# A one-hot matrix on TensorE in place of the first expert's gather

## The chip, the core and the metric

The kernel runs on one core of one Trainium2 chip. Its engines have their own instruction queues and go through them strictly in order: PE (TensorE) does matrix products, DVE (VectorE) and ACT (ScalarE) work on elements, POOL (GpSimd) does a little arithmetic and issues the indirect DMAs, SP (SyncE) issues the weight loads. The metric is the device time of one execution in microseconds (us).

## The reference

Two layers of a streaming encoder, each with three parts. Only the third part, a mixture of experts, matters here:

```python
scores = softmax(xt @ w_router + b_router)
# best group of 4 experts by the sum of its top-2 scores, then the top-2 experts in it
gate = sum(one_hot(eid, N_EXPERTS) * top_w[..., None], axis=1)
for e in range(N_EXPERTS):                       # 16 experts
    h = silu(xt @ w_gate[e]) * (xt @ w_up[e])
    y = y + gate[:, e:e + 1] * (h @ w_down[e])
x = layer_norm(DN_ALPHA * x + y)
```

xt has 512 tokens of 1024 numbers, and each token goes to two of the sixteen experts.

## The kernel before

The 512 tokens are four tiles of 128 rows, xr[0] to xr[3], in fp32. Products are made of fp16 halves: a number is scaled and split into a high half (ACT copies it to fp16, L124 or L173) and a low half (DVE subtracts the high half, L129 or L174), and three products stand for one fp32 product (`mm3`, L168 to L170).

Weights come from DRAM as units of 1 MB. `Feed` loads them in order into raw buffers (`fill`, L98, on SP's queue), and `pump` splits the next raw unit into `whi` and `wlo`. There are 4 raw buffers of the kind "b", 7 of the kind "x" and 2 of the kind "y" in this part of a layer, and 5 pairs of halves. A pair is free once PE has used it (`done`), a raw buffer once it is split. So PE frees pairs, ACT and DVE split into them, and SP loads into the raw buffers that this frees.

The stretch of the change is the passage from attention to the experts, once in each layer. `OutProj` makes the output projection tile by tile and the layer norm behind it (`ln0`, `ln`, L331 to L342). For each finished tile `x3T(t)` (L931) stores the rows to the DRAM copy `xd`, transposes them on PE and splits the result, and `logits(t)` multiplies with the router's weights. `route()` (L965) then picks the experts: some thirty small DVE operations, with one round of rank products on PE (L992, L993) that number the tokens of each expert; `pc` (L1001) holds each token's slot in its expert, `ohs` (L1005) is a one-hot matrix of the slots, 96 (`CAP`) wide.

What follows stands in this order for every engine: `tokens()` makes the list of tokens of each expert on PE and DVE (`idxT`, L1024); `fetch(0)`, `fetch(1)` and `fetch(2)` gather the rows of the first three experts from `xd` by indirect DMA on POOL (L1137); one `feed.pump(1)`; `gates(pc)` (L1030) makes the gate weights, sixteen DVE operations; `dispatch(0)` (L1152) transposes the gathered rows on PE and splits them into `xgh` and `xgl` (L1160, L173, L174); `out_rows()` (L1053) makes the rows and gates of the output on PE (`slots`, L1016) and DVE; then comes expert 0's `gate_up` (L1169).

`idle(real, rest, other)` fills PE while it would wait: in layer 0 with `real` products of the next layer's V projection (48 in all, L371; `v_end` does those that are left and splits the result), in layer 1 with `other` products that nobody reads (`warm`, L185).

Of the kernel before, what the change touches and what calls it, by code (L numbers as in the profile page):

```python
# [10 lines left out]
F16 = mybir.dt.float16  # L11
# [3 lines left out]
OP = mybir.AluOpType  # L15
# [19 lines left out]
SC = SW * SX  # L35
ISC = 1.0 / SC
RAW_B, HL_B = 4, 4
RAW_X, HL_X, RAW_Y = 7, 1, 2
YEND = 4
BIG = 4096.0  # L40
UPL = 30 + 6 * NE
# [3 lines left out]
def trunk_kernel(ctx, tc, units, xT, x, memT, alow, wa2, b_a, gn_g, w_sT, b_s, slnT,  # L45
# [20 lines left out]
    class Feed:  # L66
        def __init__(self):
            self.items = []
            self.raw = {}
            self.hl = {}  # L70
            self.nload = 0
            self.nsplit = 0
            self.rawfree = deque("b" * RAW_B)
            self.hlfree = deque("b" * HL_B)
            self.px = self.px2 = self.ph = None
            self.limit = 1 << 30

        def add(self, src, scale=SW, dest=None, cols=2048):
# [11 lines left out]
        def fill(self, eng=nc.sync):  # L90
            while self.nload < min(len(self.items), self.limit):
                k = self.slot(self.rawfree, self.nload)
                if k is None:
                    return
                src, _, _, cols = self.items[self.nload]
                pl, b = {"b": (ring, RAW_B), "x": (self.px, RAW_X), "y": (self.px2, RAW_Y), "mem": (cp, 1)}[k]
                t = pl.tile([P, 2048], F32, tag="mem" if k == "mem" else "raw", bufs=b, name=nm("raw"))
                eng.dma_start(t[:, :cols], src)  # L98
                self.raw[self.nload] = (t, k)
                self.nload += 1  # L100
# [205 lines left out]
    def transpose_x(t, hi, lo):  # L306
        for g in range(2):
            p = ps()
            for j in range(4):
                pe.transpose(p[:, j * P:(j + 1) * P], xr[t][:, (4 * g + j) * P:(4 * g + j + 1) * P], ident)  # L310
            split_ps(hi[:, 4 * g:4 * g + 4], lo[:, 4 * g:4 * g + 4],
                     p.rearrange("p (j s) -> p j s", j=4), SX)
# [114 lines left out]
    for l in range(DEPTH):  # L427
# [441 lines left out]
        with ExitStack() as ex:  # L869
# [2 lines left out]
            feed.ph = phc.__enter__()  # L872
            pxc = tc.tile_pool(name=f"px{l}", bufs=1, reuse_waits="tile")
            feed.px = pxc.__enter__()
            fin = l == DEPTH - 1
            feed.xend = {"h": u["end"], "x": u["end"] - (8 if fin else 0), "y": u["end"] - (8 if fin else YEND), "mem": u["end"]}
            feed.limit = u["end"] + 4
            feed.rawfree.extend("x" * RAW_X)
            if fin:
# [27 lines left out]
            def lay(n):  # L907
                used[0] += n
                return scr[:, used[0] - n:used[0]]
# [21 lines left out]
            def x3T(t):  # L931
                nc.scalar.dma_start(xd[t * P:(t + 1) * P, :], xr[t])
                x3hl = (ep if t % 2 else x3p).tile([P, 2, KT, P], F16, tag="xg2" if t % 2 else "x3", name=nm("x3"))
                x3[t] = (x3hl[:, 0], x3hl[:, 1])
                transpose_x(t, *x3[t])

            def logits(t):
                x3h, x3l = x3[t]
# [26 lines left out]
            def route():  # L965
                dve.tensor_reduce(c[:, :, 0], sc, axis=AX.X, op=OP.max)
                dve.tensor_tensor(sc, sc, b16(c[:, :, 0]), op=OP.subtract)
                act.activation(sc, sc, AF.Exp)
                v = sc.rearrange("p t (g e) -> p (t g) e", g=4)
                pair = lay(96).rearrange("p (g i) -> p g i", g=16)  # L970
                dve.tensor_tensor(pair[:, :, 0:3], v[:, :, 0:3], v[:, :, 1:4], op=OP.add)
                dve.tensor_tensor(pair[:, :, 3:5], v[:, :, 0:2], v[:, :, 2:4], op=OP.add)
                dve.tensor_tensor(pair[:, :, 5:6], v[:, :, 0:1], v[:, :, 3:4], op=OP.add)
                gs = small(4)
                dve.tensor_reduce(gs.rearrange("p t g -> p (t g)"), pair, axis=AX.X, op=OP.max)
                beats(zw, v)
                beats(zg, gs)
                we = wins(zw, 16)
                wg = wins(zg, NT)
                t2 = small(NE)  # L980
                tv = t2.rearrange("p t (g e) -> p (t g) e", g=4)
                gsel = scs[:, 5 * NE:6 * NE].rearrange("p (t n) -> p t n", t=NT)
                dve.scalar_tensor_tensor(gsel, wg, -1.0, th[:, 0:4], op0=OP.add, op1=OP.is_equal)
                dve.tensor_tensor(tv, we, th, op=OP.is_ge)
                gb = gsel.rearrange("p t g -> p (t g)").unsqueeze(2).to_broadcast([P, 16, 4])
                sv = sel.rearrange("p t (g e) -> p (t g) e", g=4)
                dve.tensor_tensor(sv, tv, gb, op=OP.mult)
                p = ps()
                for t in range(NT):
                    o = p[:, t * NE:(t + 1) * NE]  # L990
                    for t0 in range(t):
                        pe.matmul(o, ones16, sel[:, t0], start=(t0 == 0), stop=False)  # L992
                    pe.matmul(o, stri, sel[:, t], start=(t == 0), stop=True)  # L993
                dve.tensor_tensor(tv, we, th, op=OP.is_equal)
                dve.tensor_tensor(ch[:, 1].rearrange("p t (g e) -> p (t g) e", g=4), tv, gb, op=OP.mult)
                dve.tensor_tensor(ch[:, 0], sel, ch[:, 1], op=OP.subtract)

                used[0] = 0
                pc = lay(2 * NT * NE).rearrange("p (c x) -> p c x", c=2)
                for i in range(2):  # L1000
                    dve.scalar_tensor_tensor(pc[:, i], p[:, :NT * NE], 1.0,  # L1001
                                             ch[:, i].rearrange("p t e -> p (t e)"), op0=OP.add, op1=OP.mult)
                pch = lay(2 * NT)
                dve.tensor_reduce(pch, pc.rearrange("p c (t e) -> p (c t) e", t=NT), axis=AX.X, op=OP.add)
                dve.tensor_tensor(ohs, iot.unsqueeze(1).to_broadcast([P, 2 * NT, CAP]),  # L1005
                                  pch.unsqueeze(2).to_broadcast([P, 2 * NT, CAP]), op=OP.is_equal)
                for i in range(2):
                    dve.tensor_tensor(aux[:, i, 0], ch[:, i], b16(rid), op=OP.mult)
                return pc

            def slots(ohc, auxc, n):

# [112 lines left out]
            feed.rawfree.extend("y" * (RAW_Y - 1))  # L1125
            feed.fill()
            idle(15, 0, 15)
            pc = route()

            scat = []  # L1130

# [97 lines left out]
            def down(e, after=None):  # L1229
# [5 lines left out]
                scatter(o, idxR[:CAP, e:e + 1])  # L1235
                del E[e]

            idle(9, 0, 6)
            tokens()
            fetch(0)  # L1240
            fetch(1)
            feed.rawfree.append("y")
            feed.fill(pool)
            fetch(2)
            feed.pump(1)
            gates(pc)
            idle(11, 0, 17)
            dispatch(0)
            idle(3, 3, 3)
            v_end()  # L1250
            out_rows()
            if fin:
# [98 lines left out]
            if not fin:  # L1351
                ln_open()
                load_ln(l, 2)
                down(NE - 1)
                pxc.__exit__(None, None, None)
                phc.__exit__(None, None, None)
                with tc.tile_pool(name=f"ovf{l}", bufs=1, reuse_waits="tile") as fp:
                    overflow(fp)
            else:

                pxc.__exit__(None, None, None)
                ln_open()
                load_ln(l, 2)
# [163 lines left out]
```

## Time and profile before

| | us |
|---|---|
| median of 3 runs | 1289.42 (1288.48 to 1290.34) |
| the profiled execution, its own time | 1289.44 |
| its span in the trace | 1287.8 |
| PE busy in the span | 1175.2 (91%) |
| DVE busy in the span | 912.2 (71%) |
| ACT busy in the span | 711.9 (55%) |

The profiled execution's own time is 1.6 us above its span, and lies 0.02 us from the median of the runs. Times in the rows are counted from the start of the span. Layer 0's passage to the experts lies at about 340 to 376 us, layer 1's at about 972 to 1006 us. A timeline row gives start, duration, engine, line and operation, what is written and read, and how many such operations were merged; in brackets stands how long the engine was idle before it and what ended that.

### The profile page before, as it was taken

To read this page: it belongs to the slowest core of one execution; us is meant where nothing else is said; L and a number is where in the kernel's file an instruction comes from. 1 tells how busy PE (TensorE), PEld (TensorE's weight loads), DVE (VectorE), ACT (ScalarE), POOL (GpSimd) and SP (SyncE) were. 2 spreads that over 40 slices of the span, in tenths; PEclk is the share of its full clock that TensorE was granted. 3 is DMA by queue.
4 is the path that set the end of the run, shared out by engine and by line. 5 is a ranking of instruction groups with operands and counts; after the bars stand their busy time and mean duration, and the time that the engine had idled before them with its cause. 6 is when DMAs were issued, how large, how long until landed. Compare 5 with 4: busy or idle time off the path is not lost. (4 is left out here: it accounts for less than half of the span.)

```text
span 1287.8 us, 26082 instructions
## 1 busy us (share of the span) xinstructions
PE 1175.2 (91%) x11218; PEld 763.4 (59%) x11219; DVE 912.2 (71%) x1066; ACT 711.9 (55%) x810; POOL 235.9 (18%) x193
## 2 busy tenths in 40 slices
PE   6999999999979999999859999999998899999982
PEld 4455456464457777777645545444644777777761
DVE  3255775378578989989574275773758699899977
ACT  3435334344447888888543354232633678888873
POOL 3002000000331222231150002000004222222124
PEclk9999999999988999999879999999999899999996
DMA  9412225228569999999472231155374899999864
GB/s 360 159 67 98 98 85 178 98 98 316 208 238 345 419 418 418 418 419 394 165 291 105 98 129 36 67 207 184 110 313 142 292 377 419 417 419 418 337 235 181
DMA packets 54940, 314.76 MB, mean 244 GB/s; under 512 B 9309, under 2 KB 9405, under 8 KB 22560
## 3 DMA queue, kind: packets, MB, share of 16 engines
q1 hardware_dynamic: 42096, 279.99, 55.3%
q0 software_dynamic: 11568, 28.83, 6.2%
q10 hardware_dynamic: 1152, 4.19, 0.8%
q8 instruction: 90, 1.47, 0.5%
q14 instruction: 34, 0.28, 0.1%
HBM read 302.80 MB, written 22.68 MB: 253 GB/s over the span
## 5 line engine op out<-in xcount | busy, mean ns | idle before, releaser
L129 DVE SCALAR_TENSOR_TENSOR wlo<-raw,whi 128x2048 f16<-128x2048 f32 (+1 forms) x234 | 523.2, 2278 | 110.5 <-ACT whi L124 109.5
L124 ACT ACTIVATE whi<-raw 128x2048 f16<-128x2048 f32 (+1 forms) x239 | 441.8, 1895 | 34.7 <-PE ps L170 19.4
L169 PE MATMUL ps<-xgl,whi 128*128 128x96 f16 x2048 | 272.4, 208 | 21.8 <-DVE xgl L174 21.7
L168 PE MATMUL ps<-xgh,whi 128*128 128x96 f16 x2048 | 274.3, 208 | 5.0 <-ACT xgh L173 2.9
L170 PE MATMUL ps<-xgh,wlo 128*128 128x96 f16 x2048 | 272.6, 208 | 0.3 <-issue 0.3
L170 PEld LDWEIGHTS <-wlo 128*128 128x128 f16 x2400 | 237.8, 99 | 58.7 <-issue 25.7
L169 PEld LDWEIGHTS <-whi 128*128 128x128 f16 x2400 | 237.8, 99 | 39.2 <-issue 9.5
L168 PEld LDWEIGHTS <-whi 128*128 128x128 f16 x2400 | 238.1, 99 | 38.3 <-issue 6.7
L1143 POOL DMA_INDIRECT y<-rows,idxR x31 | 59.7, 1927 | 353.0 <-ACT rows L1233 345.0
L168 PE MATMUL ps<-whi,xT 128*128 128x512 f16 (+1 forms) x256 | 91.9, 359 | 8.4 <-ACT whi L124 7.0
L170 PE MATMUL ps<-whi,xT 128*128 128x512 f16 (+1 forms) x256 | 91.7, 358 | 3.1 <-DVE xT L174 2.2
L169 PE MATMUL ps<-wlo,xT 128*128 128x512 f16 (+1 forms) x256 | 91.7, 358 | 1.7 <-DVE wlo L129 1.7
L168 PE MATMUL ps<-whi,hhl 128*96 128x512 f16 x200 | 75.9, 380 | 2.3 <-ACT hhl L1202 2.3
L170 PE MATMUL ps<-whi,hhl 128*96 128x512 f16 x200 | 75.9, 379 | 0.0
L169 PE MATMUL ps<-wlo,hhl 128*96 128x512 f16 x200 | 75.8, 379 | 0.0
L294 ACT ACTIVATE lnmv<-lnmv,c_lneps 128x1 f32<-128x1 f32 x16 | 4.7, 295 | 111.0 <-DVE lnmv L293 111.0
L1202 ACT ACTIVATE hhl<-h 128x384 f16<-128x384 f32 x32 | 16.7, 523 | 86.5 <-DVE h L1178 86.5
L1137 POOL DMA_INDIRECT rows<-xd,idxT x22 | 49.0, 2229 | 44.7 <-PE ps L1160 15.4
L1215 PE MATMUL ps<-raw,h 128*96 128x512 f32 x112 | 50.3, 592 | 0.0
L169 PE MATMUL ps<-x2T,whi 128*128 128x512 f16 x128 | 48.5, 379 | 1.0 <-DVE x2T L174 1.0
L169 PE MATMUL ps<-wlo,mx 128*128 128x512 f16 x128 | 49.3, 385 | 0.0
L168 PE MATMUL ps<-whi,mx 128*128 128x512 f16 x128 | 49.2, 384 | 0.0
(309 smaller groups left out, 2055.3 us busy)
## 6 DMA issues: line engine op xcount, KB each, us to landing
raw<-in_units SPq DMA_DIRECT2D x249, 1024.0 KB, 11.3
xd<-xr ACTq DMA_DIRECT2D x8, 512.0 KB, 4.4
ya<-y SPq DMA_DIRECT2D x8, 512.0 KB, 6.2
yb<-y SPq DMA_DIRECT2D x8, 512.0 KB, 6.8
y<-zr SPq DMA_DIRECT2D x1, 4096.0 KB, 15.0
lng<-in_ln_g POOLq DMA_DIRECT2D x6, 512.0 KB, 5.4
lnb<-in_ln_b POOLq DMA_DIRECT2D x6, 512.0 KB, 6.8
raw<-in_xT SPq DMA_DIRECT2D x4, 512.0 KB, 6.8
```

Source lines behind the costliest of these rows:

```text
L124: act.activation(dest[0], t[:, :cols], AF.Copy, scale=scale)
L129: dve.scalar_tensor_tensor(dest[1], t[:, :cols], scale, dest[0], op0=OP.mult, op1=OP.subtract)
L168: pe.matmul(o, lh, rh, start=first, stop=False)
L169: pe.matmul(o, lh, rl, start=False, stop=False)
L170: pe.matmul(o, ll, rh, start=False, stop=last)
L294: act.activation(mvt[:, 2:3], mvt[:, 1:2], AF.Ln, bias=c_lneps, scale=(ISC * ISC if scaled else 1.0))
L1137: pool.indirect_dma_start(out=dst[:idx.shape[0], :], out_offset=None, in_=xd[:], in_offset=bass.IndirectOffsetOnAxis(ap=idx, axis=0), boun ...
L1143: i = pool.indirect_dma_start(out=y2[:], out_offset=bass.IndirectOffsetOnAxis(ap=idx, axis=0), in_=src[:CAP, :], in_offset=None, bounds_ch ...
L1202: act.activation(f2(hh), h32, AF.Copy)
L1215: pe.matmul(p[:CAP, :], E[e]["h"][:, f * CAP:(f + 1) * CAP], mv(w, f), start=(f == 0), stop=(f == 3))
```

## The change

Expert 0's rows are no longer gathered from `xd`. Four tiles `xs` hold each token tile as fp16 halves in the layout of the rows: `x3T(t)` makes the high half on ACT behind the splits of the transpose, and `halves(t)` the low half on DVE, at once for the tiles 0 to 2, and inside `route()` for tile 3. `route()` makes `p0`, the slots of expert 0, and `oh0`, their one-hot matrix, before `ohs`. A new `first_dispatch()` multiplies the `xs` halves with `oh0`: 4 tiles by 2 halves by 8 column blocks are 64 products of 128x128 with 96 columns, summed over the tiles in four PSUM banks, and copies them to `xgh` (ACT) and `xgl` (DVE). It stands ahead of `tokens()`. `fetch(0)` and `dispatch(0)` are gone, as are fillers: `idle(11, 0, 17)` and `idle(3, 3, 3)` become one `idle(5, 0, 4)`. The tiles `xs` take the room of two raw buffers of the kind "x" (7 become 5); once the products have read them, two buffers of a new kind "z" are opened in that room.

```diff
-RAW_X, HL_X, RAW_Y = 7, 1, 2
+RAW_X, HL_X, RAW_Y, RAW_Z = 5, 1, 2, 2
...
+            xs = []
+            for t in range(NT):
+                xs_ = xsp.tile([P, 2, D], F16, name=nm("xs"))
+                xs.append((xs_[:, 0], xs_[:, 1]))
...
                 transpose_x(t, *x3[t])
+                act.activation(xs[t][0], xr[t], AF.Copy, scale=SX)
+                if t < NT - 1:
+                    halves(t)
+
+            def halves(t):
+                dve.scalar_tensor_tensor(xs[t][1], xr[t], SX, xs[t][0], op0=OP.mult, op1=OP.subtract)
...
+                p0 = lay(NT)
+                pv = pc.rearrange("p c (t e) -> p c t e", t=NT)
+                dve.tensor_tensor(p0, pv[:, 0, :, 0], pv[:, 1, :, 0], op=OP.add)
+                oh0 = lay(NT * CAP // 2).bitcast(F16).rearrange("p (t c) -> p t c", t=NT)
+                dve.tensor_tensor(oh0, iot.unsqueeze(1).to_broadcast([P, NT, CAP]),
+                                  p0.unsqueeze(2).to_broadcast([P, NT, CAP]), op=OP.is_equal)
+                halves(NT - 1)
...
+            def first_dispatch():
+
+                xgh = ep.tile([P, KT, CAP], F16, tag="xgh", name=nm("xgh"))
+                xgl = ep.tile([P, KT, CAP], F16, tag="xgl", name=nm("xgl"))
+                pp = [[ps(), ps()], [ps(), ps()]]
+                for t in range(NT):
+                    for i in range(2):
+                        for k in range(KT):
+                            pe.matmul(pp[i][k // 4][:, k % 4 * CAP:(k % 4 + 1) * CAP],
+                                      xs[t][i][:, k * P:(k + 1) * P], oh0[:, t],
+                                      start=(t == 0 and k % 4 == 0), stop=(t == NT - 1 and k % 4 == 3))
+                for hf in range(2):
+                    k4 = slice(4 * hf, 4 * hf + 4)
+                    act.activation(xgh[:, k4].rearrange("p k c -> p (k c)"), pp[0][hf][:, :4 * CAP], AF.Copy)
+                    dve.tensor_copy(xgl[:, k4].rearrange("p k c -> p (k c)"), pp[1][hf][:, :4 * CAP])
+                E[0] = {"xg": (xgh, xgl)}
+
             idle(9, 0, 6)
+            first_dispatch()
             tokens()
-            fetch(0)
+            xsc.__exit__(None, None, None)
+            pzc = tc.tile_pool(name=f"pz{l}", bufs=1, reuse_waits="tile")
+            feed.pz = pzc.__enter__()
+            feed.rawfree.extend("z" * RAW_Z)
+            feed.fill()
             fetch(1)
...
             feed.pump(1)
+            idle(5, 0, 4)
             gates(pc)
-            idle(11, 0, 17)
-            dispatch(0)
-            idle(3, 3, 3)
             v_end()
             out_rows()
```

How instructions stand on DVE in layer 0 around tile 2's `x3T`, before. xr_87 is xr[2] and xr_88 is xr[3]; L303 ends tile 2's layer norm, L337 and L290 begin tile 3's, and x_324 is the transposed tile 2.

```order
L303 SCALAR_TENSOR_TENSOR xr_87<-xr_87,lnmv_2768,lnb_1481 128x1024
L337 SCALAR_TENSOR_TENSOR xr_88<-xr_88,ps_2694 128x512
L290 BN_STATS lnst_2778<-xr_88 128x6
L174 SCALAR_TENSOR_TENSOR x_324_2815<-ps_2816,x_324_2815 128x512
L174 SCALAR_TENSOR_TENSOR x_324_2815<-ps_2823,x_324_2815 128x512
L337 SCALAR_TENSOR_TENSOR xr_88<-xr_88,ps_2789 128x512
```

The same place on DVE in the changed kernel (x_326 is the transposed tile 2, xs_2446 the halves of its rows).

```order
L303 SCALAR_TENSOR_TENSOR xr_87<-xr_87,lnmv_2775,lnb_1481 128x1024
L337 SCALAR_TENSOR_TENSOR xr_88<-xr_88,ps_2699 128x512
L290 BN_STATS lnst_2785<-xr_88 128x6
L174 SCALAR_TENSOR_TENSOR x_326_2822<-ps_2823,x_326_2822 128x512
L174 SCALAR_TENSOR_TENSOR x_326_2822<-ps_2830,x_326_2822 128x512
L948 SCALAR_TENSOR_TENSOR xs_2446<-xr_87,xs_2446 128x1024
L337 SCALAR_TENSOR_TENSOR xr_88<-xr_88,ps_2796 128x512
```

One operation on 1024 columns, the low half of tile 2's rows, now stands between the splits of tile 2 and the second part of tile 3's layer norm.

On DVE from the rank products to the first of the `gates` operations (pos), layer 0, before. scr_2470 holds `pc` and what is made of it, emp and idxT are `tokens`, wlo_3066 is the low half of one weight unit.

```order
L1001 SCALAR_TENSOR_TENSOR scr_2470<-ps_3013,ch 128x64 x2
L1004 TENSOR_REDUCE scr_2470<-scr_2470 128x8
L1005 TENSOR_TENSOR ohs<-iot,scr_2470 128x768
L1008 TENSOR_TENSOR aux<-ch,rid 128x64 x2
L1023 TENSOR_SCALAR emp_3051<-ps_3042 96x16
L1024 SCALAR_TENSOR_TENSOR idxT<-ps_3042,emp_3051 96x16
L129 SCALAR_TENSOR_TENSOR wlo_3066<-raw_2445,whi_3065 128x2048
L1031 TENSOR_TENSOR pos<-scr_2470 128x64
```

The same stretch in the changed kernel, behind the rank products: L1019 is p0, L1021 is oh0, xs_2447 the low half of tile 3's rows, the two rows of L1273 the copies of `first_dispatch`, ps_3129 the products of `tokens`.

```order
L1019 TENSOR_TENSOR scr_2473<-scr_2473 128x4
L1021 TENSOR_TENSOR scr_2473<-iot,scr_2473 128x384
L948 SCALAR_TENSOR_TENSOR xs_2447<-xr_88,xs_2447 128x1024
L1025 TENSOR_REDUCE scr_2473<-scr_2473 128x8
L1026 TENSOR_TENSOR ohs<-iot,scr_2473 128x768
L1029 TENSOR_TENSOR aux<-ch,rid 128x64 x2
L1273 CAST xgl_3056<-ps_3059 128x384
L1273 CAST xgl_3056<-ps_3060 128x384
L1044 TENSOR_SCALAR emp_3138<-ps_3129 96x16
L1045 SCALAR_TENSOR_TENSOR idxT<-ps_3129,emp_3138 96x16
L129 SCALAR_TENSOR_TENSOR wlo_3158<-raw_2452,whi_3157 128x2048
L1052 TENSOR_TENSOR pos<-scr_2473 128x64
```

Five operations have come in ahead of `tokens`, and the two copies among them read what PE makes in `first_dispatch`; the weight split and `gates` still stand behind.

On ACT from the exponential of `route` (L968) on, layer 0, before. whi_3065 is the high half that the DVE row wlo_3066 needs.

```order
L968 ACTIVATE scs<-scs 128x64
L124 ACTIVATE whi_3065<-raw_2445 128x2048
L173 ACTIVATE xgh_3098<-ps_3100 128x384
L173 ACTIVATE xgh_3098<-ps_3107 128x384
L173 ACTIVATE V_2431<-ps_2903 128x512
L173 ACTIVATE V_2431<-ps_2904 128x512
```

The same place on ACT in the changed kernel; whi_3157 is that high half.

```order
L981 ACTIVATE scs<-scs 128x64
L1272 ACTIVATE xgh_3055<-ps_3057 128x384
L1272 ACTIVATE xgh_3055<-ps_3058 128x384
L124 ACTIVATE whi_3157<-raw_2452 128x2048
L173 ACTIVATE V_2431<-ps_2912 128x512
L173 ACTIVATE V_2431<-ps_2913 128x512
L124 ACTIVATE whi_3210<-raw_2454 128x2048
```

The two copies of expert 0's rows have moved from behind the weight's high half to ahead of it.

## Rows read from the trace of the kernel before

**Rows 1.** The stretch from 440 to 600 us, inside the experts of layer 0: us, busy time of each engine (instructions), granted clock of PE, DMA share, GB/s.

```profile
440.00:600.00 160.00, 151.51 (x2281) 121.09 (x2282) 145.38 (x97) 130.94 (x119) 42.23 (x20) 1.00 1.01 417
```

**Rows 2.** Who waited for whom on PE, at 330 to 400 us (first row) and at 990 to 1010 us (second row): engine and line that waited, what ended the wait, us in total, times, longest.

```profile
PE ps L1160 <- DMA rows<-xd,idxT: 5.6, 1, 5.6
...
PE ps L1160 <- DMA rows<-xd,idxT: 4.7, 1, 4.7
```

**Rows 3.** The timeline of PE in layer 0 behind the rank products and the nine V products of `idle(9, 0, 6)`: `tokens` (L1016), the transposes of `dispatch(0)` (L1160), the last five products of `out_rows` (L1016).

```profile
362.26 0.78 PE L1016 MATMUL ps<-aux,ohs 128*96 128x16 f16 x8
...
371.02 1.54 PE L1160 MATMUL ps<-ident,rows 96*128 96x96 f32 x8 [5.58 <-DMA rows<-xd,idxT]
...
374.29 0.57 PE L1016 MATMUL ps<-aux,ohs 128*96 128x48 f16 x5
```

**Rows 4.** The timeline of PE in expert products of 128x128 with 96 columns: the first product of layer 0's expert 0, then the first and the last of 23 products in a row, then the first and the last of 57 products in a row, of a later expert.

```profile
374.69 0.25 PE L168 MATMUL ps<-xgh,whi 128*128 128x96 f16 x1
374.75 0.28 PE L169 MATMUL ps<-xgl,whi 128*128 128x96 f16 x1
...
376.51 0.25 PE L170 MATMUL ps<-xgh,wlo 128*128 128x96 f16 x1
...
420.01 0.21 PE L169 MATMUL ps<-xgl,whi 128*128 128x96 f16 x1
...
422.39 0.21 PE L168 MATMUL ps<-xgh,whi 128*128 128x96 f16 x1
```

**Rows 5.** The timeline of DVE in layer 0, the rows on which the working rests.

```profile
337.45 0.69 DVE L337 SCALAR_TENSOR_TENSOR xr<-xr,ps 128x512 f32<-128x512 f32 x1 [1.67 <-PE ps L170]
...
344.07 1.29 DVE L174 SCALAR_TENSOR_TENSOR x<-ps,x 128x512 f16<-128x512 f32 x2 [0.92 <-ACT x L173]
345.28 0.68 DVE L337 SCALAR_TENSOR_TENSOR xr<-xr,ps 128x512 f32<-128x512 f32 x1
...
359.50 0.35 DVE L1001 SCALAR_TENSOR_TENSOR scr<-ps,ch 128x64 f32<-128x64 f32 x2
...
360.21 0.96 DVE L1005 TENSOR_TENSOR ohs<-iot,scr 128x768 f16<-128x768 f32 x1
...
363.37 2.28 DVE L129 SCALAR_TENSOR_TENSOR wlo<-raw,whi 128x2048 f16<-128x2048 f32 x1
365.57 0.22 DVE L1031 TENSOR_TENSOR pos<-scr 128x64 f32<-128x64 f32 x1
...
368.55 0.19 DVE L1045 TENSOR_TENSOR aux<-aux 128x64 f16<-128x64 f16 x1
372.48 1.20 DVE L174 SCALAR_TENSOR_TENSOR xgl<-ps,xgh 128x384 f16<-128x384 f32 x2 [3.74 <-ACT xgh L173]
...
375.89 11.10 DVE L129 SCALAR_TENSOR_TENSOR wlo<-raw,whi 128x2048 f16<-128x2048 f32 x5
386.91 0.55 DVE L1178 SCALAR_TENSOR_TENSOR h<-ps,h 128x384 f32<-128x384 f32 x1
```

**Rows 6.** The timeline of ACT in layer 0: the splits of tile 2, the weight unit behind the exponential, expert 0's copies, and the first weight units behind `dispatch(0)`.

```profile
343.46 1.06 ACT L173 ACTIVATE x<-ps 128x512 f16<-128x512 f32 x2
...
355.75 1.89 ACT L124 ACTIVATE whi<-raw 128x2048 f16<-128x2048 f32 x1
371.96 0.49 ACT L173 ACTIVATE xgh<-ps 128x384 f16<-128x384 f32 x1 [14.31 <-PE ps L1160]
...
377.82 5.94 ACT L124 ACTIVATE whi<-raw 128x2048 f16<-128x2048 f32 x3 [0.16 <-issue]
```

**Rows 7.** Groups of instructions by line and shape: ACT's and DVE's half of a split of 128x1024; count, busy us and mean ns of one.

```profile
L124 ACT ACTIVATE xT<-raw 128x1024 f16<-128x1024 f32 x4 | 4.2, 1056 | 8.0 <-DMA raw<-in_xT 8.0
...
L129 DVE SCALAR_TENSOR_TENSOR xT<-raw,xT 128x1024 f16<-128x1024 f32 x4 | 4.9, 1225 | 9.6 <-ACT xT L124 9.6
```

**Rows 8.** The timeline of layer 1's passage, by engine: four rows of DVE, one of ACT, five of PE (L185 are the six fillers behind the rank products).

```profile
977.15 1.29 DVE L174 SCALAR_TENSOR_TENSOR x<-ps,x 128x512 f16<-128x512 f32 x2 [0.87 <-ACT x L173]
...
990.77 0.36 DVE L1001 SCALAR_TENSOR_TENSOR scr<-ps,ch 128x64 f32<-128x64 f32 x2
...
998.63 0.19 DVE L1045 TENSOR_TENSOR aux<-aux 128x64 f16<-128x64 f16 x1
...
1010.40 6.70 DVE L129 SCALAR_TENSOR_TENSOR wlo<-raw,whi 128x2048 f16<-128x2048 f32 x3 [2.43 <-ACT whi L124]
...
1008.46 1.91 ACT L124 ACTIVATE whi<-raw 128x2048 f16<-128x2048 f32 x1 [3.14 <-PE ps L170]
...
990.22 1.46 PE L185 MATMUL ps<-ones 128*128 128x512 f16 x6
...
1001.48 1.51 PE L1160 MATMUL ps<-ident,rows 96*128 96x96 f32 x8 [4.68 <-DMA rows<-xd,idxT]
...
1004.07 0.81 PE L1016 MATMUL ps<-aux,ohs 128*96 128x48 f16 x8
1004.70 0.25 PE L168 MATMUL ps<-xgh,whi 128*128 128x96 f16 x1
```

**Rows 9.** Two stretches of PE behind the wait for the gather, one in each layer: us, busy time (instructions), granted clock as a share of 2.4 GHz, DMA share, GB/s.

```profile
374.60:376.00 1.40, 1.40 (x21) 0.50 0.45 129
...
1006.00:1008.00 2.00, 2.00 (x28) 0.50 0.06 14
```

**Rows 10.** Issue to landing of weight units (L98) at 560 to 612 us, in us.

```profile
DMA to landing us min/median/max: 10.8/19.0/21.1
```

More of the change, by code (lines that the diff above doesn't have):

```diff
@@ L74, in __init__ @@
             self.hlfree = deque("b" * HL_B)
-            self.px = self.px2 = self.ph = None
+            self.px = self.px2 = self.pz = self.ph = None
             self.limit = 1 << 30
@@ L95, in fill @@
                 src, _, _, cols = self.items[self.nload]
-                pl, b = {"b": (ring, RAW_B), "x": (self.px, RAW_X), "y": (self.px2, RAW_Y), "mem": (cp, 1)}[k]
+                pl, b = {"b": (ring, RAW_B), "x": (self.px, RAW_X), "y": (self.px2, RAW_Y), "z": (self.pz, RAW_Z), "mem": (cp, 1)}[k]
                 t = pl.tile([P, 2048], F32, tag="mem" if k == "mem" else "raw", bufs=b, name=nm("raw"))
@@ L874, in trunk_kernel @@
             feed.px = pxc.__enter__()
+            xsc = tc.tile_pool(name=f"xs{l}", bufs=1, reuse_waits="tile")
+            xsp = xsc.__enter__()
+            xs = []
+            for t in range(NT):
+                xs_ = xsp.tile([P, 2, D], F16, name=nm("xs"))
+                xs.append((xs_[:, 0], xs_[:, 1]))
             fin = l == DEPTH - 1
-            feed.xend = {"h": u["end"], "x": u["end"] - (8 if fin else 0), "y": u["end"] - (8 if fin else YEND), "mem": u["end"]}
+            feed.xend = {"h": u["end"], "z": u["end"] - (8 if fin else 0), "x": u["end"] - (8 if fin else 0), "y": u["end"] - (8 if fin else YEND), "mem": u["end"]}
             feed.limit = u["end"] + 4
@@ L1008, in route @@
                     dve.tensor_tensor(aux[:, i, 0], ch[:, i], b16(rid), op=OP.mult)
-                return pc
+                return pc, oh0
             def slots(ohc, auxc, n):
@@ L1127, in trunk_kernel @@
             idle(15, 0, 15)
-            pc = route()
+            pc, oh0 = route()
             scat = []
@@ L1354, in trunk_kernel @@
                 down(NE - 1)
+                pzc.__exit__(None, None, None)
                 pxc.__exit__(None, None, None)
@@ L1359, in trunk_kernel @@
             else:
+                pzc.__exit__(None, None, None)
                 pxc.__exit__(None, None, None)
```

## The prediction

> **What bounds the kernel now.** I read first a long stretch inside the experts, to learn whether a later start there can be made up; then the waits on PE at the passage to the experts; then the timelines of PE, DVE and ACT there, to see which operation each engine stands at.
>
> Inside the experts DVE is busy 145.4 of 160 us, PE's modelled time 151.5, the DMA share is full at 417 GB/s [rows 1]. The weight units still land at most 21.1 us after issue late in the phase [rows 10], and 13 raw buffers of 1 MB are 13 x 1.05 / 0.417 = 33 us of loading; so data waits for the splits and not the splits for data. PE, ACT and DVE follow one another there without slack: a start that is later or earlier by some us is carried to the end of the layer one to one.
>
> At the passage PE waits 5.6 us in layer 0 and 4.7 us in layer 1 for the gather of expert 0 [rows 2]. This is what the change can win. But more than the gather lies ahead of expert 0's first product. On PE the products of `out_rows` stand directly before it [rows 3, 8], and they read what `gates` makes on DVE. Before, `gates` was done at 368.74 (layer 0) and 998.82 (layer 1) [rows 5, 8], long before the gathered rows had come, so it cost nothing. The order rows show that the change puts PE's 64 products, two ACT copies, a weight split and then `gates` into one line.
>
> **The change part by part.** I follow layer 0 by the times of before, each term as a shift.
>
> *The row halves.* Eight ACT copies of 128x1024 at 1.06 us and eight DVE operations at 1.23 us [rows 7], four of each in a layer. For tile 2 ACT ends the splits at 343.46 + 1.06 = 344.52 and the copy at 345.6; DVE's low half then ends at 346.8. Behind it is tile 3's second norm part, which started at 345.28 [rows 5, 6] and now at 346.8: +1.5 us. Everything to the route hangs on that norm, so the rank products' result on DVE ends at 361.35 and not 359.85. For tiles 0 and 1 the shift is covered: behind tile 1's splits the second norm part of tile 2 waits 1.67 us for PE [rows 5]; if that cover is gone, a few tenths more. Tile 3's copy on ACT lies between its splits and the exponential, which waits for DVE.
>
> *The one-hot matrix.* p0 is a small operation, about 0.2 us (L1031's 0.22 [rows 5]). oh0 is half of `ohs`, whose row has 0.96 for 768 columns: between 0.2 and 0.96, I take 0.5. It is there at 362.1, tile 3's low half at 363.3. `ohs` and what follows come 2 us later in addition, but stay hidden behind PE's products.
>
> *The 64 products.* PE comes to them behind the nine V products, at 362.26 + 1.5 = 363.8 [rows 3]. They have the shape of the expert's own: 22 intervals in 1.76 us are 0.080 each at half rate, 56 in 2.38 us are 0.0425 at full rate [rows 4]. So 64 cost between 2.7 and 5.1 us. PE has just idled before the rank products and comes back slowly; the nine V products use up most of that, so I take 3.0, near the full rate: end at 366.8.
>
> *The new line behind them.* ACT's two copies of 128x384 at 0.49 [rows 6], the first while the low halves are still being made: end at 367.4. Before, ACT made the next weight unit's high half at 355.75, in time that cost nothing [rows 6]; now it stands behind the copies and takes 1.89, to 369.3. DVE's copies (0.6 each, from the pair of 1.20) and `idxT` are done by 368.3, so its weight split waits for ACT: 2.28, to 371.6. `gates` takes 368.74 - 365.57 = 3.17 [rows 5], to 374.8, the eight products of `out_rows` 0.8 [rows 8], to 375.6. Expert 0's first product was at 374.69 [rows 4]: **+0.9 us**. The wait for the gather is gone and PE now waits as long for `gates`.
>
> *What comes off.* Eight transposes of 1.5 us [rows 3], the split of the gathered rows, one gather. They were ahead of the same point, so their price is already in the difference. The V products lost from `idle` are done in `v_end`, 12 in all behind `tokens`, by 370, in the new wait.
>
> *The clock.* PE comes out of a wait at half its rate: the clock is 0.50 in expert 0's first stretch in either layer [rows 9]. Layer 0's restart was at 371.02 [rows 3], and full rate came at 376.5 [rows 4], 24 products into the expert. Now PE restarts at 374.8 with the products of `out_rows`, so some 25 more products run at 0.080 in place of 0.0425: the first weight unit is used up at about 379.5 and not 377.7. The weight units after it wait for that pair of halves: ACT took the next at 377.82 [rows 6]. DVE's five splits from 375.89 [rows 5] start 0.85 later, and the third of them now waits for ACT until 381.4, another 0.3. Layer 0: **+1.2 us**.
>
> The Trainium skill (TensorE: Matmul & The Clock Gate, "HAM oscillation — how this bites in real kernels") says that a long pause of PE is paid twice, by the wait and by matmuls at half clock behind it, so a change that only swaps the cause of the pause wins nothing of the second price. By it the half rate is the 0.3 us above; if the new pause left the clock alone, layer 0 would come to a gain, which is the last rival below. Rows 9 show 0.50 behind the gather.
>
> *Layer 1.* Here PE's fillers are at full rate and end at 991.68 + 1.5 = 993.2 [rows 8]. The rank result ends at 991.13 + 1.5 = 992.6 [rows 8], oh0 at 993.4, the 64 products at 0.0425 at 996.2. Then copies to 996.8, high half to 998.7, low half to 1001.0, `gates` to 1004.2, `out_rows` to 1005.0, against 1004.70 [rows 8]: +0.3. ACT's next unit waits for expert 0's first pair (1008.46 [rows 8]), now 1008.85, and for up to 12 more products at half rate behind it. Between +0.3 and +0.9, I take **+0.6**.
>
> *The raw buffers.* Two units come at 367 and not with the first seven at about 300. They are the last to be loaded ahead of the experts, and by the order of the loads some eight units of 2.2 us each are split before them behind 375, so they have 10 us and more to land. Price nothing; the bound is two loads, 2 x 1.05 / 0.417 = 5 us in a layer. The gathers of experts 1 and 2 come 4 us later, with expert 1's rows needed only behind expert 0's products, near 385: nothing.
>
> The sum: 1.2 + 0.6 = +1.8 us on the profiled execution's 1289.44, which is the median within 0.02. **1291.2 us**, 0.14% above before. A measurement of this kernel cannot tell less than about 0.2%, 2.6 us, from no change.
>
> **The rivals.** *The gather was the only thing PE waited for (faster).* Then expert 0 starts when its copies are made, 367.9 and 997.2, a gain of 6.8 + 7.5 us: 1275. For it: the wait rows name the gather alone [rows 2]. Against: the order on PE, with `out_rows` ahead of the expert in both kernels. A part of it would come if the weight split were out of the way of `gates`: 4 us less in a layer. 10% with its parts.
>
> *The 64 products and the start of expert 0 run at half rate (slower).* Place: `first_dispatch` in both layers. All at 0.080 adds 2.1 us in layer 0 and 2.4 in layer 1, with the copies, split and gates behind: 1295.7. It decides from half the products on, where 0.8 us more take the sum past 0.2%. For: PE idles before the rank products and is at half rate in this stretch now. Against: in layer 1 fillers run right up to it. 25%.
>
> *The raw buffers run out (slower).* If expert 0 finds its weights late, up to 5 us a layer: 1299 with half of that. Against it is the count above. 5%.
>
> *The pause becomes too short for the clock to fall.* Then expert 0 starts at 0.0425 from its first product: layer 0 gains 24 x 0.0375 = 0.9 on before, layer 1 41 x 0.0375 = 1.5, about what the new line costs: 1289. 7%. The page named above has the pause's length decide this; rows 9 show falls behind pauses of 5.6 and 4.7, and the new ones are 4.8 and 6.
>
> **How the numbers follow.** The forecast has 53%, its own range 1289.5 to 1293 by the bounds of oh0, the products and layer 1. Four fifths need part of the faster and slower rivals: 1286.5 to 1295.7. Faster by over 0.2%: the first rival's 10% and 4% for a better hidden line, 14%. Slower: 25 + 5 and a little of the forecast's upper end, 31%. Within 0.2%: 55%.
>
> **What would show it.** Right: no PE wait for a gather, but a wait of 4 to 6 us for `gates` on DVE ahead of `out_rows`; the second half of tile 3's norm 1.5 us later against tile 2's splits; the copies, the weight's high half, its low half and `gates` back to back with no idle time; expert 0's first product within 1.5 us of before, counted from tile 2's norm. Wrong: `out_rows` not waiting on DVE, the low half of the weight unit done before the copies, or ACT waiting for raw units in the first experts.

## The result and the profile after

The changed kernel takes 1296.08 us (median of 6 runs, 1294.71 to 1296.9), the kernel before beside it 1289.64: a ratio of 1.0052, with a 95% interval of 1.0038 to 1.0067. It is slower by 0.5%, or 6.4 us; the forecast was +1.8 us, and the end of its range 1295.7. The profiled run took 1296.15 us, its span is 1294.5 us.

The forecast's first sign was that the second half of tile 3's norm would start 1.5 us later, behind tile 2's low half. These are DVE's rows of layer 0 in the changed kernel (start, duration, line, operation), for the norm parts (L337), the splits (L174) and the low halves (L948):

```profile
333.24 1.29 DVE L174 SCALAR_TENSOR_TENSOR x<-ps,x 128x512 f16<-128x512 f32 x2 [8.28 <-ACT x L173]
334.67 3.34 DVE L948 SCALAR_TENSOR_TENSOR xs<-xr,xs 128x1024 f16<-128x1024 f32 x1
337.94 0.67 DVE L337 SCALAR_TENSOR_TENSOR xr<-xr,ps 128x512 f32<-128x512 f32 x1
...
339.25 0.67 DVE L337 SCALAR_TENSOR_TENSOR xr<-xr,ps 128x512 f32<-128x512 f32 x1
...
345.86 1.29 DVE L174 SCALAR_TENSOR_TENSOR x<-ps,x 128x512 f16<-128x512 f32 x2 [0.92 <-ACT x L173]
347.30 3.28 DVE L948 SCALAR_TENSOR_TENSOR xs<-xr,xs 128x1024 f16<-128x1024 f32 x1
350.50 0.67 DVE L337 SCALAR_TENSOR_TENSOR xr<-xr,ps 128x512 f32<-128x512 f32 x1
```

The low halves of tiles 1 and 2 took 3.34 and 3.28 us, not 1.23. The row at 339.25 is the second norm part of tile 2; before, it started at 337.45 after a wait of 1.67 us for PE [rows 5]. That wait is gone and it is 1.8 us late, so the cover counted on for tile 1 is broken. The last row answers to the one at 345.28 [rows 5]: **+5.2 us, not +1.5**.

The profile shows no wait of DVE ahead of these two operations. What they have in common is seen on another engine. POOL's timeline in the same stretch:

```profile
332.86 4.07 POOL L127 TENSOR_TENSOR wlo<-raw,whi 128x2048 f16<-128x2048 f32 x1 [33.77 <-ACT raw L126]
345.43 4.07 POOL L127 TENSOR_TENSOR wlo<-raw,whi 128x2048 f16<-128x2048 f32 x1 [8.49 <-ACT raw L126]
```

These are the two weight splits that `feed.pump(1, True)` gives to POOL. They end at 336.93 and 349.50, and DVE's low halves end 1.08 us later each, at 338.01 and 350.58: about the time that a free low half takes. The view of the tile `xs` shows that the others were free (minimum, median and maximum in ns; eight in all, four of them under POOL):

```profile
L948 DVE SCALAR_TENSOR_TENSOR xs<-xr,xs x8: 1217/2252/3345, 316.9 to 1001.2; 128x1024 f16<-128x1024 f32 x8
```

Operations that read PSUM and only one operand from SBUF were not held: the splits (L174) at 345.86, under POOL's second split, took their usual 1.29 us the pair, and in the kernel before the norm part at 345.28 [rows 5] took 0.68 under a POOL split of 343.64 to 347.72. The Trainium skill (SBUF — State Buffer, "🔬 SBUF: two separate sides") states this rule: a DVE operation with two SBUF inputs and a GpSimd (POOL) operation that reads SBUF exclude each other, and the loser waits for the whole instruction of the other. By that rule the rows above follow.

The passage behind the route went as forecast, or better. PE's rows of layer 0, from the 64 products (L1267) to expert 0's first product (L168), and that product in layer 1:

```profile
366.13 2.88 PE L1267 MATMUL ps<-scr,xs 128*128 128x96 f16 x64
368.85 0.49 PE L1037 MATMUL ps<-aux,ohs 128*96 128x16 f16 x8
...
376.93 0.83 PE L1037 MATMUL ps<-aux,ohs 128*96 128x48 f16 x8 [4.98 <-DVE aux L1066]
377.59 0.25 PE L168 MATMUL ps<-xgh,whi 128*128 128x96 f16 x1
...
1012.87 0.25 PE L168 MATMUL ps<-xgh,whi 128*128 128x96 f16 x1
```

The rank result on DVE, in layer 0 and in layer 1:

```profile
364.72 0.36 DVE L1014 SCALAR_TENSOR_TENSOR scr<-ps,ch 128x64 f32<-128x64 f32 x2
...
1000.18 0.35 DVE L1014 SCALAR_TENSOR_TENSOR scr<-ps,ch 128x64 f32<-128x64 f32 x2 [0.23 <-PE ps L1006]
```

The gather's wait [rows 2] is gone, and PE waits 4.98 us for `gates` (L1066), in layer 1 6.74. From the end of the rank result to expert 0's first product it is 377.59 - 365.08 = 12.5 us, where it was 374.69 - 359.85 = 14.8 [rows 4, 5]. In layer 1 it is 1012.87 - 1000.53 = 12.3, where it was 1004.70 - 991.13 = 13.6 [rows 8]. So the change does win something at the passage, 2.3 and 1.3 us, and loses 5.2 us ahead of it, in each layer.

### The profile page after: what moved, and what is told of

It reads as the page before. It is cut to its first block, busy times and chain, and to the rows that moved or that the text cites. A ratio compares the mean times of both kernels' runs of the same rounds, so it can differ in the third digit from the quotient of the medians.

```text
span 1294.5 us, 26295 instructions
## 1 busy us (share of the span) xinstructions
PE 1173.8 (91%) x11311; PEld 765.0 (59%) x11312; DVE 928.3 (72%) x1078; ACT 719.3 (56%) x818; POOL 229.9 (18%) x191
## 5 line engine op out<-in xcount | busy, mean ns | idle before, releaser
L168 PE MATMUL ps<-xgh,whi 128*128 128x96 f16 x2048 | 274.1, 208 | 6.6 <-PEq L1301 3.7
L168 PEld LDWEIGHTS <-whi 128*128 128x128 f16 x2400 | 237.9, 99 | 40.0 <-issue 10.4
L168 PE MATMUL ps<-whi,xT 128*128 128x512 f16 (+1 forms) x256 | 92.2, 360 | 8.8 <-ACT whi L124 7.3
L168 PE MATMUL ps<-whi,hhl 128*96 128x512 f16 x200 | 75.9, 380 | 2.3 <-ACT hhl L1223 2.3
L1158 POOL DMA_INDIRECT rows<-xd,idxT x20 | 44.2, 2209 | 46.0 <-PE ps L1181 23.8
L168 PE MATMUL ps<-whi,mx 128*128 128x512 f16 x128 | 49.2, 384 | 0.0
```

The source lines that it names most:

```text
L168: pe.matmul(o, lh, rh, start=first, stop=False)
L1158: pool.indirect_dma_start(out=dst[:idx.shape[0], :], out_offset=None, in_=xd[:], in_offset=bass.IndirectOffsetOnAxis(ap=idx, axis=0), boun ...
```

## The experiments

Theory: the loss is the collision of DVE's low halves with POOL's splits. Rivals: it is the line of copies, weight split and gates behind the products, or the clock that TensorE is granted. All line numbers are those of the kernel in question. The table collects layer 0 from the timelines of the profiled runs. Its first column is where the run stood, against before, when DVE began tile 1's splits (333.18 before); executions differ from it there by up to 1.3 us. The other columns are shifts against before with that taken off, in us.

```
                              entry  tile 3's norm  expert 0's first  expert 1's gating  median us, ratio to before (95%)
changed                       +0.06      +5.16            +2.83             +1.63        1296.08  1.0052 (1.0038 to 1.0067)
low halves moved              -0.82      +0.11            -0.13             -1.57        1287.83  0.9989 (0.9976 to 1.0002)
row halves with the gather    -0.22      +5.18            +6.20             +5.16        1302.71  1.0094 (1.0069 to 1.0119)
gates first                   +0.38      +5.16            -1.05             +0.74        1292.55  1.0024 (1.0008 to 1.0040)
moved, and gates first        -0.62      +0.12            -4.14             -2.49        1284.53  0.9970 (0.9957 to 0.9984)
one SBUF input                +0.26      +2.33             0.00             -1.25        1290.16  1.0002 (0.9985 to 1.0019)
gather, low halves moved      +0.37      +0.12            +1.52             -0.97        1292.52  1.0026 (1.0011 to 1.0040)
POOL's split in pieces        -0.11      +1.65            -1.06             -1.72        1289.00  0.9992 (0.9977 to 1.0008)
moved, gates first, pieces    +1.32      +0.11            -4.04             -2.37        1283.39  0.9952 (0.9935 to 0.9968)
```

**The low halves moved.** Nothing is taken out; two calls stand elsewhere.

```diff
-                if t < NT - 1:
+                if t == 0:
                     halves(t)
...
             op_.ln0(3)
+            halves(1)
...
             logits(2)
+            halves(2)
```

> The changed kernel with the low halves of tiles 1 and 2 moved out of the way of POOL's weight splits: tile 1's behind the first norm part of tile 3, tile 2's behind tile 2's logits. Theory (the loss is that these two DVE operations took 3.3 us each under POOL's split, in place of 1.2): all eight low halves take about 1.2 us, the second half of tile 3's norm starts within 0.6 us of the kernel before in layer 0 (345.28), expert 0 starts 1.5 to 2 us earlier than before, and the time is 1285 to 1289 us, below the kernel before. Rival (the loss is the line of copies, weight split and gates behind the 64 products, or the clock; the late norm would have been absorbed): the low halves may be short, but the time stays at 1294 to 1296 us.

Measured: 1287.83 us, some 8 us less than the changed kernel and not to be told from the kernel before. The norm is on time (+0.11). Expert 0's first product, though, came 0.13 us earlier and not the 1.5 to 2 that were expected: the nine V products ahead of the 64 took 3.6 us, with a granted clock of 0.50 at 360 to 362 us, where they took 1.9 in the changed kernel. All eight low halves are short:

```profile
L948 DVE SCALAR_TENSOR_TENSOR xs<-xr,xs x8: 1206/1212/1221, 316.1 to 990.1; 128x1024 f16<-128x1024 f32 x8
```

Now tile 1's low half comes first, and POOL is the one to wait. The rows of DVE, then those of POOL, in the same run:

```profile
342.25 1.21 DVE L948 SCALAR_TENSOR_TENSOR xs<-xr,xs 128x1024 f16<-128x1024 f32 x1
...
353.40 1.85 DVE L980 TENSOR_TENSOR scs<-scs,cr 128x64 f32<-128x64 f32 x1
```

```profile
342.81 4.58 POOL L127 TENSOR_TENSOR wlo<-raw,whi 128x2048 f16<-128x2048 f32 x1 [6.76 <-ACT raw L126]
350.71 4.45 POOL L127 TENSOR_TENSOR wlo<-raw,whi 128x2048 f16<-128x2048 f32 x1 [3.31 <-ACT raw L126]
```

The first of these POOL splits takes 4.58 us and not 4.07. The second one meets the tiny L980, ahead of the route, which takes 1.85 us (0.22 in layer 1, where no split runs) and ends 0.09 us after POOL.

**Only the row halves.** The gather path of expert 0 is back; the one-hot matrix and the 64 products are left out, and the row halves are made for nobody.

```diff
...
-            first_dispatch()
             tokens()
...
+            fetch(0)
             fetch(1)
...
             feed.pump(1)
-            idle(5, 0, 4)
             gates(pc)
+            idle(11, 0, 17)
+            dispatch(0)
+            idle(3, 3, 3)
```

> The changed kernel with the gather of expert 0 through DRAM, its split and its transposes put back, and the 64 products and the one-hot matrix of the first expert left out: what is left of the change is the row halves (made, but read by nothing) and the division of the raw buffers. Theory (the low halves under POOL cost 5.2 us at tile 3's norm in each layer, carried on one to one): 1297 to 1301 us, slower than the changed kernel too. By the sizes of the prediction (1.5 us in each layer): 1291 to 1294 us. Rival (the loss is the line behind the 64 products): 1290 us, as before.

Measured: 1302.71 us (four of the six runs at 1302.7, two at 1298.5), some 13 us above the kernel before and above the theory's own range. The loss stays when the products and the line behind them are gone, so it comes with the row halves; that it is larger than twice 5.2 us is not explained. The norm is 5.18 late and expert 1's gating 5.16, one to one. PE waits for the gather again, 6.6 us in layer 0 and 4.7 in layer 1:

```profile
PE ps L1175 <- DMA rows<-xd,idxT: 6.6, 1, 6.6
```

**The gates first.** The low halves stay where they collide; `gates` stands ahead of the weight split on DVE.

```diff
+            gates(pc)
             feed.pump(1)
             idle(5, 0, 4)
-            gates(pc)
```

> The changed kernel with the gates computed ahead of the weight split that followed the copies on DVE, the low halves left where they collide. Theory: two costs stand in a row, the collision (5.2 us at tile 3's norm) and the line behind the products; this edit takes only the second, PE's wait of 4.98 us for the gates falls to about 1.7 and expert 0's first product comes 2 to 3.3 us earlier in each layer: 1290 to 1292 us. Rival (the weight split is needed by expert 0 just then, so that a split made 3 us later is waited for in place of the gates): 1295 to 1297 us.

Measured: 1292.55 us, 3.5 us less than the changed kernel, a bit short of the theory. PE's waits of layer 0 show why (the line that waited, what ended the wait, us, times, longest); first the changed kernel, then this one:

```profile
PE ps L1037 <- DVE aux L1066: 5.0, 1, 5.0
...
PE ps L169 <- DVE xgl L174: 1.5, 1, 1.5
```

```profile
PE ps L169 <- DVE xgl L174: 5.1, 1, 5.1
...
PE ps L1037 <- DVE aux L1066: 1.4, 1, 1.4
```

The wait for the gates fell by 3.6 us, and the next one, for expert 1's rows, grew by 3.6. DVE has the same work to do in either order, up to expert 0's gating; the edit saved DVE little more than the 1.05 us in which it waited for ACT's high half. In layer 0 expert 1's gating came 0.9 us earlier by the table. In layer 1, where the wait fell from 6.7 to 3.3, it came 3.3 us earlier against the route. So layer 0 went nearly as the rival has it, with DVE's queue in place of the gates, and layer 1 as the theory has it.

**Both.** The two edits together.

> Both edits: low halves of tiles 1 and 2 moved as in the first of these kernels, gates ahead of the weight split. Theory (the two costs add, since one lies ahead of the route and the other behind it): the gains add, 1279 to 1284 us, faster than the kernel before. Rival (DVE is full, so that what is moved comes back as a later split): 1286 to 1289 us, no better than the first of these kernels.

Measured: 1284.53 us, 0.3% below the kernel before (0.9970, 0.9957 to 0.9984). From the changed kernel's ratio of 1.0052 the two edits take 0.0063 and 0.0028 alone and 0.0082 together: most of each adds, and the time is just above the range that the theory gave.

**One SBUF input.** It leaves out the subtraction in tiles 1 and 2.

```diff
             def halves(t):
+                if t == 1:
+                    return dve.tensor_copy(xs[t][1], xr[t])
+                if t == 2:
+                    with nc.allow_low_precision(reason='one element'):
+                        return dve.tensor_reduce(xs[t][1], xr[t].unsqueeze(2), axis=AX.X, op=OP.add)
```

> The changed kernel with other DVE operations at the places where the low halves of tiles 1 and 2 collide with POOL's weight split: tile 1 gets a plain copy of the residual rows (one SBUF input), tile 2 a reduction over a length of one (one SBUF input, another kind of operation). It leaves out the subtraction in these two tiles. Theory (POOL's split holds up DVE operations that read two operands from SBUF, as the low half does, and not those with one): both take at most their 1024 columns, about 1.2 us, and the time falls to 1287 to 1291 us. Rival (any DVE operation on SBUF of this size is held up while POOL works): both take 3 us or more and the time stays at 1295 to 1297 us. The Trainium skill (SBUF - State Buffer, two separate sides) has the copy held as well, by its rule on fp32 copies in a performance mode, and the reduction not: then only tile 1's takes 3 us.

Measured: 1290.16 us. The rows of the tile, over both layers, then POOL's splits in layer 0:

```profile
L949 DVE CAST xs<-xr x2: 3032/3036/3039, 334.6 to 968.9; 128x1024 f16<-128x1024 f32 x2
L952 DVE TENSOR_REDUCE xs<-xr x2: 1208/1208/1209, 346.7 to 980.9; 128x1024 f16<-128x1024 f32 x2
```

```profile
333.07 4.07 POOL L127 TENSOR_TENSOR wlo<-raw,whi 128x2048 f16<-128x2048 f32 x1 [33.77 <-ACT raw L126]
345.10 4.08 POOL L127 TENSOR_TENSOR wlo<-raw,whi 128x2048 f16<-128x2048 f32 x1 [7.96 <-ACT raw L126]
```

The reduction started at 346.74 in the midst of a POOL split (345.10 to 349.18) and took 1.21 us; the copy was held to 337.69, 0.55 us after POOL's end at 337.14. So both expectations of my own were wrong in part: one SBUF input alone doesn't save an operation. It is as the Trainium skill has it (the section named above), that an fp32 copy in a performance mode is locked out too. The 0.55 us left after POOL's end are about half of the reduction's time, as a faster mode would have it; no run here shows this copy by itself.

**The gather, with the low halves moved.** The edits of the first two runs together.

> The run with the gather path put back (row halves made but unread, no one-hot products), now with the low halves of tiles 1 and 2 moved out of POOL's way. Theory (the row halves cost 5.2 us a layer by the collision alone; well placed, with raw buffers 5 and 2 in place of 7, they cost under 0.5 us a layer): 1289 to 1292 us against 1302.7 with the halves in the way. Rival (the row halves cost something besides, by ACT's copies or by the raw buffers taken from the loads): 1295 us or more.

Measured: 1292.52 us, 10 us less than with the halves in the way, and at the edge of what was expected: 0.26% (0.11 to 0.40%) above the kernel before. Up to the norm the row halves cost 0.12 us. Where the rest of some 3 us arises stays open: the profiled run of this version was its fastest, 1290.02. With the low halves placed alike, the products in place of the gather win about 0.4% (0.9989 against 1.0026).

**POOL's split in pieces.** The low halves stay where they collide.

```diff
-                    pool.tensor_tensor(dest[1], t[:, :cols], dest[0], op=OP.subtract)
+                    for c in range(0, cols, 512):
+                        pool.tensor_tensor(dest[1][:, c:c + 512], t[:, c:c + 512], dest[0][:, c:c + 512],
+                                           op=OP.subtract)
```

> The changed kernel with POOL's weight split cut into four instructions of 512 columns, everything else as it was, the low halves where they collide. Theory (DVE is locked out for the whole of a POOL instruction): the low half of a tile waits at most for one piece, about 1.0 us, and takes 1.2 to 2.3 us in place of 3.3; tile 3's second norm part comes about 3 to 4 us earlier, and the time is 1288 to 1293 us. Rival (the two engines share the bandwidth of a port, each slowed in proportion): the pieces change nothing, 3 us and more, 1295 to 1297 us.

Measured: 1289.00 us. DVE's low half of tile 1 and POOL's four pieces beside it:

```profile
334.50 1.54 DVE L950 SCALAR_TENSOR_TENSOR xs<-xr,xs 128x1024 f16<-128x1024 f32 x1
```

```profile
332.69 5.49 POOL L128 TENSOR_TENSOR wlo<-raw,whi 128x512 f16<-128x512 f32 x4 [33.77 <-ACT raw L126]
```

The low half waits some 0.3 us for the piece that is running, and then POOL waits for it: 5.49 us for the four pieces, where four pieces that meet no low half take 4.50 (the third split of this run). A shared bandwidth, the rival, would have left the low half at 3 us and more; the holding goes by instruction. Without one instruction of DVE or PE moved, tile 3's norm is 3.5 us earlier and 7 us of the time are gone. The 1.65 us by which the norm is still late are close to the +1.5 that was forecast for low halves that nobody holds.

**All three, and the controls.** The changed kernel, both edits, and both edits with POOL's pieces, on one chip; the version with pieces ran once before that.

> Low halves moved, gates ahead of the weight split, and POOL's weight splits cut in four. Theory: the third weight split of layer 0, which now holds up one small DVE operation ahead of the route until it ends (1.85 us for L980, 0.22 where POOL is idle), holds it for at most 1.0 us; the scale operation of tile 3's norm (2.35 us for two halves, 1.41 where POOL is idle) gets a little shorter as well: about 1 us in layer 0 and 0.5 in layer 1 off the version without pieces, 1282 to 1284 us. Rival (four instructions cost POOL and DVE more changes of the port than they save): 1285 us or more.

> The changed kernel itself, on one chip with the two versions below, since the experiments were compared with it only through the kernel before. Theory: 1294 to 1298 us, ratio to the kernel before 1.003 to 1.008. If it came out at 1290, a part of what the experiments seemed to win would be the difference of chips.

> Low halves moved and gates first, beside the changed kernel on one chip. Theory: 10 to 13 us below it, 1283 to 1286 us.

> The same with POOL's splits in four pieces, on the same chip, to see whether the pieces still win anything once the low halves are out of the way. Theory: 0.5 to 1.5 us less than without pieces. Rival: no difference, since the same DVE time is only cut up.

Measured: 1283.39 us for the version with pieces at first (0.9952). On the one chip: changed 1295.45 (1.0054, 1.0034 to 1.0074), both edits 1284.09 (0.9953, 0.9938 to 0.9967), with pieces 1283.42 (0.9952, 0.9938 to 0.9965). So the loss and the gain hold on other chips. The pieces add nothing that can be told once the low halves are out of the way: the operation that met POOL's third split then took 1.17 us and the next one 0.78, together about the 1.85 and 0.21 of the version without pieces. The times of all four runs lie within what was expected of them, though the last cannot tell its theory (0.5 to 1.5 us less) from its rival (no difference). The best version is the changed kernel with the low halves moved and the gates first, 11 us below the changed kernel on the same chip and some 4 to 6 below the kernel before.

## Why the prediction was wrong

*The step that failed* is "The row halves": DVE operations "at 1.23 us [rows 7]", with tile 1's "covered" by PE's wait. The 1.23 was taken from a split at the start of the kernel, where POOL runs no split, and the sum leaves out what POOL does at the place to which the operation goes. There POOL holds DVE for 2.1 us, twice in each layer. Tile 1 then costs 1.8 us and tile 2 another 3.4. The term was +1.5 in each layer and measured +5.2: an error of 3.7 us twice, 7.4 us, where the total missed by 4.9. The run with the row halves alone has the whole of the 5.2, and moving the low halves takes it away (0.11 left), POOL's pieces all but 1.65 us of it.

The trace of before showed it. Two rows of DVE there are too long:

```profile
346.96 1.97 DVE L300 SCALAR_TENSOR_TENSOR xr<-xr,lnmv,lng 128x512 f32<-128x512 f32 x2
...
354.10 1.45 DVE L967 TENSOR_TENSOR scs<-scs,cr 128x64 f32<-128x64 f32 x1
...
356.00 0.20 DVE L972 TENSOR_TENSOR scr<-scs 128x32 f32<-128x32 f32 x1
```

```profile
343.64 4.08 POOL L127 TENSOR_TENSOR wlo<-raw,whi 128x2048 f16<-128x2048 f32 x1 [6.76 <-ACT raw L126]
351.41 4.06 POOL L127 TENSOR_TENSOR wlo<-raw,whi 128x2048 f16<-128x2048 f32 x1 [3.69 <-ACT raw L126]
355.42 1.83 POOL L1116 MEMSET rows<- 128x1024 f32 x2
```

The pair of L300 takes 1.41 in the changed kernel, where POOL is idle, and the small L967, which works on 64 columns, took 1.45 (0.23 in layer 1) and ended 0.08 us after POOL. An operation of 64 columns that takes longer than one of 1024 is the mark. POOL's MEMSETs, which read nothing, held nobody: L972, with two operands from SBUF, took 0.20 us beside them and 0.20 in layer 1 without them.

*The one-hot matrix* took 0.56 (0.5), *the 64 products* 2.88 in either layer (3.0 and 2.7). They started sooner than forecast in layer 0, since the V products ahead of them ran at the full rate: 12.5 us from the rank result to expert 0, where the forecast comes to 14.25. In layer 1 it is 12.3 against 12.4.

*The new line* came as told, each behind the other: DVE's split waits 1.05 us for ACT, `gates` follows, PE waits 4.98. The clock's +0.3 came too: ACT's next weight unit (380.97) started 3.38 us behind expert 0's first product, where it was 3.13 [rows 4, 6]. But PE's wait was not the whole price, as the gates-first run shows: in layer 0 DVE's queue sets expert 1's rows whatever its order. Between expert 0 and expert 1, 1.2 us of the delay were made up (2.83 to 1.63), which I had not counted: between the two gatings DVE waited 2.3 us for ACT's high halves, where it waited 3.4 before. Why it waited less stays open.

*Carried one to one*: right from expert 1 on. The shift in layer 0 is 1.7 us at expert 1's gating and at the last expert's, in layer 1 it is 7.5 at both. Of the 7.5, 4.2 stood there at tile 1's splits already, so layer 1 adds 3.2. Between the layers the first profile loses another 2.5 us, a part of it in a stretch at the lower clock (1.2 GHz; the granted clock is 0.91 at 800 to 820 us, 1.00 before). In the second profile of the same kernel that loss is absent up to tile 3's norm of layer 1, but there the rank result comes 1.5 us later instead. Behind the late norm PE waits 4.1 us for tile 3's rows (1.2 before), the granted clock is 0.50 from 988 to 996 us, and 15 fillers take 6.1 us where they took 3.4. So the late norm can cost once more by way of the clock; in the first profile it did not, the rank result being as late as the norm in either layer. How much of the 6.4 us the clock takes is not shown.

*The rivals.* That 64 products would run at half rate was the one I gave 25%; they did not. That the measured time lies near its 1295.7 is chance: another mechanism made it. That the gather was all that PE waited for did not come about: with the gates out of the way of the weight split, 3.5 of the 14.3 us came. No wait of ACT for raw units showed up at the passage; the sum of that rival is off besides, since half of 5 us in each layer on 1291.2 is 1296.2 and not 1299. Nor did the pause become too short for the clock to fall: the granted clock was 0.50 at 378 to 380 us. It did in the gates-first run, where PE waited 1.4 us and the granted clock was 1.00 at 376 to 378.

## What to carry to other kernels

Before an operation is put on DVE, look at POOL's timeline at that very place, and take its price from a row that stood beside the same neighbour: in these runs a DVE operation that reads two operands from SBUF, and an fp32 copy, stood still until the POOL split beside it had ended (3.34 us in place of 1.22, and 3.04). A small DVE operation that takes as long as a large one and ends just behind a POOL instruction is the mark of it. Then move it to a place where POOL is idle, or cut POOL's instruction, before touching the line that the change was about.

## What was not expected of the hardware

The holding goes in both directions and by instruction: 3.34 us in place of 1.22 for DVE behind POOL, 4.58 in place of 4.07 for POOL behind DVE, and 1.54 with POOL's work in four pieces.

The clock behind one and the same pause. In two runs of the version with both edits PE waited 2.25 us ahead of the rank products, doing the same before and after it. The granted clock behind it (the stretch of 360 to 362 us; us, busy us and count by engine, granted clock, DMA share, GB/s), first in one run, then in the other:

```profile
360.00:362.00 2.00, 2.00 (x6) 0.76 (x5) 1.97 (x4) 0.00 (x0) 0.00 (x0) 0.50 0.95 397
```

```profile
360.00:362.00 2.00, 1.84 (x18) 1.01 (x19) 1.73 (x8) 0.00 (x0) 0.00 (x0) 1.00 1.03 434
```

It was 1.2 GHz in the one and 2.4 in the other. The first run was 1.55 us ahead at the rank products; its nine V products took that much longer, and both ran their 64 products from 362.35 and 362.36. So here the clock ate up the early start; how much of the spread between executions comes this way is not shown.
